# A hybrid attention layer: the input projection as a phase of its own by seven block products, neighbourhood heads first, half of the output projection among the differential units

## The chip, the core and the metric

The kernel runs on one core of a Trainium2 chip. The time is device microseconds (us) of one execution. The engines are named as in the profile: PE (TensorE matmul), PEld (its weight load), DVE (VectorE), ACT (ScalarE), POOL (GpSimd) and SP (SyncE, which here issues every DMA).

## What is computed

One layer on 1024 tokens of width 1024, in float32: a SwiGLU block, a mixer of two kinds of attention heads, a second SwiGLU block, each with a residual and a layer norm. The change is in the mixer.

```python
def hybrid_mixer(h, w_in, w_out, ...):            # h: (1, 1024, 1024), w_in: (1024, 3072)
    p = h @ w_in
    na_q, na_k, na_v, df_q, df_k, df_v = jnp.split(p, splits, axis=-1)      # 512 columns each
    na_out = neighbourhood_attention(na_q, na_k, na_v, na_rpb)   # 8 heads of 64, 16 x 64 token grid,
                                                                 # 8 x 16 window, bias table per head
    df_out = differential_attention(df_q, df_k, df_v, lam, ...)  # 4 heads, softmax1 - lam * softmax2 over
                                                                 # all 1024 keys, ALiBi, RMS norm
    return jnp.concatenate([na_out, df_out], axis=-1) @ w_out    # w_out: (1024, 1024)
# layer: x = LN1(a*x + 0.5*SwiGLU_1(x)); x = LN2(a*x + hybrid_mixer(x)); x = LN3(a*x + 0.5*SwiGLU_2(x))
```

## The kernel before

Every large product is made of three matmuls on a value split into a high and a low part (hi x hi, hi x lo, lo x hi; `mm3`, and L568 to L570 in the projection). `split` makes the two parts: a cast on ACT (L66) and a subtraction on DVE or POOL (L67). The layer-normed x lies transposed in `xq` as four blocks (A11, A12, A21, A22: two halves of tokens by two halves of the width).

The kernel runs through these stages. `gate_up` (first SwiGLU) takes 22 column tiles: for most of them it uses seven block products of 4 k-steps (Strassen-Winograd: 7 x 12 = 84 matmuls of 512 columns) in place of eight (96). `down_phase` follows and ends in row blocks (`Rows.down`, 24 matmuls, layer norm and 8 transposes into `xq` for each of 8 row blocks).

Then the mixer. Its heads form eight groups of 128 columns: four differential ("df") heads, then four pairs of neighbourhood ("na") heads. `project(g)` makes K, V and Q of one group by plain products: 3 matrices x 2 token halves x 24 = 144 matmuls, 1152 in all. It is a generator that stops after each 3 matmuls. The first group's projection runs alone; the other seven are fed by `Filler` into the units of the group before, so that 3 matmuls of the next group stand at each `fill()` in the program. A df unit is one block of 128 queries of one head (32 units): `df_scores` (8 matmuls, two additions with a row minimum on DVE at L682, two exponentials on ACT, a reciprocal and two combinations on DVE), `df_transpose` (8 transposes, casts and subtractions) and, for each two units, `df_out` (24 matmuls of 256 columns, a norm). An na unit is 128 queries of a pair of heads (32 units): `na_scores` (4 matmuls, L822 on DVE, exponentials on ACT, a scaling on POOL at L828), two units later `na_transpose` (6 transposes), three units later `na_out` (12 small matmuls). The bias tables are loaded by `na_raw` (16 DMAs per group) and built by `na_tables` (12 POOL instructions per group, L793). V is transposed on PE (`df_v` L663, `na_v` L803). In the last na group there is nothing left to project, and the units run without filler; the loads of the output weights and of the attention outputs (`load_o`) are issued in it.

The output projection follows: attention outputs come back from DRAM (`oTd`), 8 k-steps, 384 matmuls, in two passes over the row blocks, the second with LN2. Then the second SwiGLU.

The program is ordered per engine ahead of time: buffers come from pools that are opened and closed with the stages, an instruction waits when its buffer is still read by an earlier stage that used the same memory, and each engine and the SP queue takes its list in order.

## Time and profile before

| | |
|---|---|
| Runs (median, lowest, highest of 3) | 1962.92, 1962.77, 1968.08 us |
| Profiled execution: time, span | 1969.43 us, 1967.7 us |
| PE, DVE, ACT, POOL busy in the span | 1926.4 (98%), 1217.6 (62%), 762.3 (39%), 208.8 (11%) us |
| Matmul instructions in the span | 9152 |
| DMA, busy share of 16 engines | 39.3% on the queue that SP issues to |

Busy time is the union of an engine's instructions. Matmuls overlap, so that the time of one (some 390 ns for 512 columns) is longer than the step from one to the next; the step is read from the starts in the timeline. The stages of the mixer begin at about 679 us (first projection alone), 712.6 (df units), 1003.4 (na units) and 1205.3 us (output projection).

### The profile page before, as it was taken

To read this page: it belongs to the slowest core of one execution; us is meant where nothing else is said; L and a number is where in the kernel's file an instruction comes from. 1 tells how busy PE (TensorE), PEld (TensorE's weight loads), DVE (VectorE), ACT (ScalarE), POOL (GpSimd) and SP (SyncE) were. 2 spreads that over 40 slices of the span, in tenths; PEclk is the share of its full clock that TensorE was granted. 3 is DMA by queue.
4 is the path that set the end of the run, shared out by engine and by line. 5 is a ranking of instruction groups with operands and counts; after the bars stand their busy time and mean duration, and the time that the engine had idled before them with its cause. 6 is when DMAs were issued, how large, how long until landed. Compare 5 with 4: busy or idle time off the path is not lost.

```text
span 1967.7 us, 24088 instructions
## 1 busy us (share of the span) xinstructions
PE 1926.4 (98%) x9152; PEld 1562.2 (79%) x9152; DVE 1217.6 (62%) x1823; ACT 762.3 (39%) x1228; POOL 208.8 (11%) x188
## 2 busy tenths in 40 slices
PE   9999999999999999999999999999999999999998
PEld 7777887877887878888777777887787888878887
DVE  8575655545555956778663346787666646455557
ACT  5333333334333245556544455133333333344331
POOL 0000000000001312011044443100000000000005
PEclk9999999999999999999999999999999999999999
DMA  4556323248762331112122226224555222387632
GB/s 168 208 203 222 120 102 118 102 166 300 235 196 88 106 91 41 49 41 62 30 56 67 64 65 226 83 89 160 192 205 191 93 102 99 125 294 254 195 119 86
DMA packets 90771, 266.26 MB, mean 135 GB/s; under 512 B 11680, under 2 KB 15648, under 8 KB 82976
## 3 DMA queue, kind: packets, MB, share of 16 engines
q1 hardware_dynamic: 90656, 264.73, 39.3%
q8 instruction: 72, 1.18, 0.2%
q14 instruction: 43, 0.35, 0.1%
HBM read 183.42 MB, written 72.88 MB: 130 GB/s over the span
## 4 chain that ended last, share of the span: by engine, by line
PE 42%; DMA 3%; DVE 3%; ACT 1%; issue 1%; POOL 0%; SPq 0%; POOLq 0%; DVEq 0%; ACTq 0%
PE psA L80 5%; PE psA L82 5%; PE psA L81 5%; PE psA L435 5%; PE psB L435 4%; PE psB L80 3%; PE psB L81 3%; PE psB L82 3%; PE psB L568 2%; PE psB L570 2%; PE psB L569 2%; PE psB L851 2%; PE psA L818 1%; DMA wr<-in_wgu 1%; PE psB L843 1%
## 5 line engine op out<-in xcount | busy, mean ns | idle before, releaser
L80 PE MATMUL psA<-x,wsp 128*128 128x512 f32 x448 | 181.5, 405 | 8.8 <-ACT t L377 5.3
L80 PE MATMUL psA<-s,wsp 128*128 128x512 f32 x480 | 189.6, 395 | 0.0
L82 PE MATMUL psA<-s,wsp 128*128 128x512 f32 x480 | 187.4, 390 | 0.0
L81 PE MATMUL psA<-s,wsp 128*128 128x512 f32 x480 | 186.7, 389 | 0.0
L66 ACT CAST wsp<-wr 128x1024 fp32r<-128x1024 f32 x124 | 128.9, 1049 | 128.9 <-DVE wr L205 121.3
L81 PE MATMUL psA<-x,wsp 128*128 128x512 f32 x448 | 175.8, 392 | 0.5 <-DVE x L67 0.5
L82 PE MATMUL psA<-x,wsp 128*128 128x512 f32 x448 | 175.1, 391 | 0.0
L568 PE MATMUL psB<-x,wsp 128*128 128x512 f32 x384 | 160.5, 418 | 0.0
L67 DVE TENSOR_TENSOR wsp<-wr,wsp 128x1024 fp32r<-128x1024 f32 x124 | 149.5, 1223 | 12.9 <-ACT wsp L66 12.9
L570 PE MATMUL psB<-x,wsp 128*128 128x512 f32 x384 | 152.2, 396 | 0.0
L569 PE MATMUL psB<-x,wsp 128*128 128x512 f32 x384 | 150.9, 393 | 0.0
L67 POOL TENSOR_TENSOR wsp<-wst,wsp 128x1024 fp32r<-128x1024 f32 x28 | 67.6, 2415 | 759.3 <-ACT wsp L66 759.3
L67 DVE TENSOR_TENSOR hd<-wst,hd 128x1024 fp32r<-128x1024 f32 x84 | 102.0, 1223 | 73.0 <-ACT hd L66 68.2
L204 DVE TENSOR_TENSOR wr<-wr 128x1024 f32<-128x1024 f32 x40 | 49.0, 1225 | 148.6 <-DMA wr<-in_wgu 148.6
L66 ACT CAST hd<-wst 128x1024 fp32r<-128x1024 f32 x84 | 87.7, 1054 | 124.7 <-PE psA L435 36.3
L66 ACT CAST wsp<-wst 128x1024 fp32r<-128x1024 f32 (+1 forms) x90 | 93.0, 1034 | 105.5 <-DMA wst<-in_wd 27.9
L67 DVE TENSOR_TENSOR wsp<-wst,wsp 128x1024 fp32r<-128x1024 f32 (+1 forms) x62 | 73.8, 1190 | 84.1 <-ACT wsp L66 76.0
L80 PEld LDWEIGHTS psA<-x,wsp 128*128 128x128 f32 x448 | 84.1, 188 | 45.4 <-ACT t L377 16.1
L435 PE MATMUL psA<-hd 128*128 128x512 f32 x504 | 116.2, 389 | 0.0
L144 POOL TENSOR_TENSOR mv<-mv,cols 128x1 f32<-128x1 f32 x24 | 35.5, 1478 | 721.1 <-DVE mv L143 721.1
L435 PEld LDWEIGHTS psA<-hd 128*128 128x128 f32 x504 | 94.6, 188 | 19.7
L80 PEld LDWEIGHTS psA<-s,wsp 128*128 128x128 f32 x480 | 90.0, 188 | 25.4 <-ACT sg L394 8.2
(183 smaller groups left out, 4096.4 us busy)
## 6 DMA issues: line engine op xcount, KB each, us to landing
wr<-in_wgu SPq DMA_DIRECT2D x42, 1024.0 KB, 4.8
hSd<-hs SPq DMA_DIRECT2D x18, 1792.0 KB, 5.7
wst<-hSd SPq DMA_DIRECT2D x126, 256.0 KB, 3.6
wst<-wTd SPq DMA_DIRECT2D x72, 256.0 KB, 3.7
wst<-in_wd SPq DMA_DIRECT2D x54, 256.0 KB, 4.8
wst<-in_w_in SPq DMA_DIRECT2D x24, 512.0 KB, 3.4
wt<-in_wd SPq DMA_DIRECT2D x18, 512.0 KB, 3.7
wt<-in_wd SPq DMA_DIRECT2D x36, 256.0 KB, 5.4
```

The source lines that it names most:

```text
L66: A.copy(hi, x)
L67: eng.tensor_tensor(lo, x, hi.bitcast(FT), OP.subtract)
L80: T.matmul(ps, ah, bh, start=start and j == 0, stop=False, skip_group_check=skip)
L81: T.matmul(ps, ah, bl, start=False, stop=False, skip_group_check=skip)
L82: T.matmul(ps, al, bh, start=False, stop=j == n - 1, skip_group_check=skip)
L144: G.tensor_tensor(mv[:, 3:4], mv[:, 2:3], mhalf[:, 0:1], OP.pow)
L204: V.tensor_tensor(l[:, 0:4:3], l[:, 2:4], l[:, 3:5], OP.subtract)
L435: T.matmul(banks[T_], o[:, x, a], o[:, w, 512:1024], start=start and p == 0 and j == 0, stop=p == NP - 1 and j == 2, skip_group_check=not ...
L568: T.matmul(ps, hi, xh, start=k == 0, stop=False)
L569: T.matmul(ps, hi, xl, start=False, stop=False)
L570: T.matmul(ps, lo, xh, start=False, stop=k == KT - 1)
L851: T.matmul(po[64 * j:64 * j + 64, c % 2], Vc[0:w, r + k, 64 * j:64 * j + 64], PTs[j][0:w, k], start=k == 0, stop=k == 2)
```

## The change

All of K, V and Q is projected first, into DRAM. The gate-up code becomes a class `Seven` that takes what to do with its results; `KQ` runs it over 8 column tiles (K as the "gate" and Q as the "up" of each group: 2 plain tiles of 96 and 6 of 84 matmuls) and writes hi and lo parts to `kqd`. V follows in seven products of 48 matmuls with x as the stationary operand, so that it comes out with tokens on the partitions; its weight sums are made among the KQ tiles (`wVd`), the results go to `vdd` (hi and lo, df heads) and `vnd` (na heads). `project`, both transposes of V and `oTd` go.

The four na groups run before the four df heads. They have no filler. K, Q and V are loaded from DRAM (`load_k` 4 DMAs per group, `load_q` 8, `na_v` 16, `load_v` 2). Attention outputs are split at once into the blocks of `xq`, which the projection no longer needs. The na half of the output projection (`out_na`, 64 pieces of 3 matmuls, with the residual) is the filler of the df units; its sums go to DRAM as `x1e`. The output stage then has the 4 k-steps of the df heads, 192 matmuls.

```diff
-    oTd = dr.tile([8, P, S], FT, name="oTd")
+
+    x1e = dr.tile([8, P, DM], FT, name="x1e")
+    kqd = [dr.tile([P, 2, 2, 2, 512], FT, name=f"kqd{h}") for h in range(8)]
+    wVd = dr.tile([P, 4, 4, 512], FT, name="wVd")
+    vdd = dr.tile([P, 2, 8, 512], FT, name="vdd")
+    vnd = dr.tile([S, 512], FT, name="vnd")
...
+        def put(s, f, j, t, x):
+            o = s.c.dv.tile([P, 2, 512], FR, name="dv")
+            hi, lo = o[:, 0], o[:, 1]
+            if j == 0:
+                A.activation(hi, x, AF.Copy, scale=k_scale(f))
+                V.scalar_tensor_tensor(lo, x, k_scale(f), hi.bitcast(FT), OP.mult, OP.subtract)
+            else:
+                if f < 4:
+                    x, hi, lo = by_columns(x), in_order(hi), in_order(lo)
+                split_back(hi, lo, x)
+            dma(kqd[f][:, j, :, t], o.bitcast(FT))
...
+        def plain(s, f, t, ps):
+            for j in range(2):
+                s.put(f, j, t, ps[:, j])
+
+        def add(s, f, j, t, x, ps):
+            to = s.c.u[:, t] if j else s.c.sg[:, t]
+            V.tensor_tensor(to, x, ps, OP.add)
+            s.put(f, j, t, to)
+
...
+            if f == 7:
+                s.ops.append(fetch_v(len(s.ops)))
+            elif i == 4 and 1 <= f < 5:
+                l = s.wt.tile([P, 7, 512], FT, name="wt")
+                dma(l[:, 1:5], I["wv"].rearrange("p (b k c) -> p b k c", b=4, k=4)[:, :, f - 1])
+                sum4(l)
+                for b, x in enumerate((l[:, 0:1], l[:, 3:4], l[:, 5:7])):
+                    dma(wVd[:, b:b + x.shape[1], f - 1], x)
...
+    W0, load0 = first_weights(I["wkq"])
+    for j in range(2):
+        for k in (0, 4):
+            load0(j, k, 4)
+    with ExitStack() as es:
+        c = Seven(es, 2)
+        kq = KQ(c)
+        c.run(I["wkq"], 8, kq, W0, None, kq.begin, kq.hook)
+        ops = kq.ops
...
+        def put_df(t, T_, x):
+            o = c.dv.tile([P, 2, 512], FR, name="dv")
+            split_back(o[:, 0], o[:, 1], x)
+            dma(vdd[:, :, 4 * t + T_], o.bitcast(FT))
+
+        def put_na(t, x, banks):
+            for T_ in range(4):
+                o = wst.tile([P, 1024], FT, name="wst")[:, 0:512]
+                V.tensor_tensor(o, x[T_], banks[T_], OP.add)
+                dma(vnd[(4 * t + T_) * P:(4 * t + T_ + 1) * P], o)
+
+        A_ = [psA.tile([P, 2, 512], FT, name="psA") for _ in range(2)]
+        A_ = [x[:, i] for x in A_ for i in range(2)]
+        product(0, A11, A_, True)
+        p1 = copies(A_, [c.t() for _ in range(4)])
+        B_ = four()
+        product(1, A12, B_, True)
+        for T_ in range(4):
+            V.tensor_tensor(p1[T_], p1[T_], B_[T_], OP.add)
+            put_df(0, T_, p1[T_])
+        product(2, c.S2, A_, False)
+        u2 = copies(A_, [x[:, i] for x in (c.u, c.sg) for i in range(2)])
+        C_ = four()
+        product(3, A21, C_, True)
+        p5 = copies(C_, [c.t() for _ in range(4)])
+        product(4, c.S3, A_, False)
+        put_na(1, p5, A_)
+        product(5, c.S4, C_, False)
+        put_na(0, u2, C_)
+        product(6, A22, A_, False)
+        for T_ in range(4):
+            put_df(1, T_, A_[T_])
...
-            wk, wv, wq = (split_w(I["w_in"][c]) for c in (ck, cv, cq))
...
-        PIECES = 48
-        groups = [dict(kind="df", h=h) for h in range(4)] + [dict(kind="na", h=h) for h in range(4)]
-
-        def filler(i, places):
-            return Filler(project(groups[i]) if i < 8 else nothing(), PIECES, places)
...
+        def load_k(g):
             K = g["K"] = kp.tile([P, 2, S], FR, name="K")
...
+            for j in range(2):
+                a, b = slice(64 * j, 64 * j + 64), slice(64 - 64 * j, 128 - 64 * j)
+                for to, i in ((a, 0), (b, 1)):
+                    dma(K[to, j].bitcast(FT).rearrange("p (t c) -> p t c", t=2), kqd[g["f"]][a, 0, i])
+
+        def load_q(g, t):
+            Q = qp.tile([P, 2, 2, 512], FR, name="Q")
+            g["Q"].append(Q)
+            for j in range(2):
+                a, b = slice(64 * j, 64 * j + 64), slice(64 - 64 * j, 128 - 64 * j)
+                for to in (a, b):
+                    dma(Q[to, j].bitcast(FT), kqd[g["f"]][a, 1, :, t])
...
+            def na_v(g, c):
+                c0, nc_, _ = NA_C[c]
+                Vc = vp.tile([P, 4, P], FT, name="Vc")
+                rows = vnd.rearrange("(r c) d -> r c d", c=GW)
+                for k in range(4):
+                    dma(Vc[0:4 * nc_, k], rows[4 * k:4 * k + 4, c0:c0 + nc_, g["h"] * P:(g["h"] + 1) * P])
+                return Vc
...
+                        if r == 1 and c == 3:
+                            for t in range(2):
+                                split(*xk(t, g["h"]), g["oT"][:, t * 512:(t + 1) * 512], V)
...
+            g = groups[0]
+            na_raw(g)
+            na_tables(g, 0, V)
+            load_q(g, 1)
+            for i in range(4):
+                g, nxt = groups[i], groups[i + 1]
+                g["oT"] = op_.tile([P, S], FT, name="oT2")
+                g["V"] = g["V"] if i else [na_v(g, c) for c in range(4)]
+                wo.append(split_w(I["w_out"][i]))
+                for r in range(2):
+                    tabs = g["tab"]
+                    for c in range(4):
+                        es_ = na_scores(g, r, c, tabs)
+                        if c == 1:
+                            if r == 0:
+                                na_tables(g, 1)
+                                if i < 3:
+                                    na_raw(nxt)
+                                load_k(nxt)
+                                load_q(nxt, 0)
+                            elif i < 3:
+                                na_tables(nxt, 0)
+                        if r == 1:
+                            if i < 3:
+                                nxt.setdefault("V", []).append(na_v(nxt, c))
+                            if c == 2:
+                                load_q(nxt, 1)
+                        queue.append(dict(g=g, r=r, c=c, e=es_, V=g["V"][c], age=-1))
+                        advance()
+            while queue:
+                advance()
...
+            def load_v(g):
...
+                for i in range(2):
+                    dma(Vt[:, i].bitcast(FT), vdd[:, i, :, g["h"] * P:(g["h"] + 1) * P])
...
-                    dma(oTd[4 + g["h"], :, qq * 256:(qq + 1) * 256], oT)
+                    o = slice(qq % 2 * 256, qq % 2 * 256 + 256)
+                    hi, lo = (x[:, o] for x in xk(qq // 2, 4 + g["h"]))
+                    split(hi, lo, oT, V)
...
+            def out_na():
+
+                for tb in range(8):
+                    y = yt.tile([P, DM], FT, name="yt")
+                    dma(y, x1d[tb])
+                    for dh in range(2):
+                        ds_ = slice(dh * 512, (dh + 1) * 512)
+                        ps = psB.tile([P, 512], FT, name="psB")
+                        for k in range(4):
+                            (ah, al), w = o_part(k)(tb), wo[k]
+                            for j, (x, i) in enumerate(((ah, 0), (ah, 1), (al, 0))):
+                                T.matmul(ps, x, w[:, i, ds_], start=k == 0 and j == 0, stop=k == 3 and j == 2)
+                            if k == 3:
+                                V.scalar_tensor_tensor(y[:, ds_], y[:, ds_], ALPHA, ps, OP.mult, OP.add)
+                                if dh:
+                                    dma(x1e[tb], y)
+                            yield
...
+            units = [(g, qb) for g in groups[4:8] for qb in range(8)]
...
+            load_v(groups[4])
+            fill = Filler(out_na(), 64, 92)
...
-            dma(m.y[t], x1d[t])
-            if t < 4:
-                load_o(4 + t)
-                wo.append(split_w(I["w_out"][src[4 + t]], wo_p, "wo", V if t == 1 else G))
+            dma(m.y[t], x1e[t])
+        wo = [split_w(I["w_out"][4 + k], *((wo_p, "wo") if k > 1 else ())) for k in range(4)]
...
-        hs = [o_part(k) for k in range(8)]
-        m.down(hs[0:2], wo[0:2], ALPHA)
-        m.down(hs[2:8], wo[2:8], 1.0, post2)
+        m.down([o_part(4 + k) for k in range(4)], wo, 1.0, post2)
```

## Rows read from the trace of the kernel before

**Rows 1.** Busy time by stage: us, PE, PEld, DVE, ACT, POOL; clock, DMA share, GB/s.
```profile
640.00:679.00 39.00, 39.00 (x217) 33.77 (x217) 37.46 (x64) 8.68 (x14) 9.34 (x7) 0.98 0.23 89
679.00:712.60 33.60, 33.60 (x155) 27.94 (x154) 12.25 (x18) 9.18 (x15) 10.50 (x5) 1.00 0.46 133
712.60:1003.40 290.80, 285.44 (x1566) 236.12 (x1566) 213.53 (x453) 170.97 (x336) 42.18 (x28) 1.00 0.17 49
1003.40:1205.30 201.90, 195.88 (x1196) 152.89 (x1194) 94.71 (x286) 100.72 (x279) 92.75 (x116) 0.98 0.26 74
1205.30:1307.00 101.70, 101.70 (x520) 86.20 (x519) 71.40 (x111) 18.78 (x30) 18.99 (x11) 1.00 0.35 127
```

**Rows 2.** Timeline of PE, row blocks, and first product after the output stage: start, us.
```profile
647.53 0.39 PE L82 MATMUL psB<-hd,wsp 128*128 128x512 f32 x1
...
652.32 0.39 PE L82 MATMUL psB<-wsp,hd 128*128 128x512 f32 x1
652.55 1.03 PE L161 MATMUL psA<-ident,y 128*128 128x128 f32 x8
...
658.89 1.04 PE L161 MATMUL psA<-ident,y 128*128 128x128 f32 x8
...
1300.20 0.47 PE L80 MATMUL psA<-x,wsp 128*128 128x512 f32 x1
```

**Rows 3.** Timeline, second gate-up: PE's wait at its entry; one DVE addition, two tiles apart.
```profile
1364.03 0.50 PE L80 MATMUL psA<-x,wsp 128*128 128x512 f32 x1 [1.24 <-DVE u L386]
...
1551.15 0.68 DVE L373 TENSOR_TENSOR sg<-t,psB 128x512 f32<-128x512 f32 x1
...
1589.94 0.68 DVE L373 TENSOR_TENSOR sg<-t,psB 128x512 f32<-128x512 f32 x1
```

**Rows 4.** Groups on DVE, df stage: shapes, count, busy us, mean ns, idle before.
```profile
L682 DVE CUSTOM_DVE_ANT_0 e<-psA,dist 128x1024 f32<-128x1024 f32 x64 | 76.9, 1220 | 1.0
L689 DVE SCALAR_TENSOR_TENSOR e<-e,st 128x1024 f32<-128x1024 f32 x32 | 45.2, 1414 | 1.0
L700 DVE TENSOR_TENSOR aT<-psB,aT 128x512 fp32r<-128x512 f32 x63 | 41.8, 685 | 1.9 <-ACT aT L699 1.8
L604 DVE TENSOR_TENSOR Q<-psB,Q 64x512 fp32r<-64x512 f32 x18 | 12.3, 686 | 12.0 <-ACT Q L603 11.9
L582 DVE SCALAR_TENSOR_TENSOR K<-psB,K 64x512 fp32r<-64x512 f32 x16 | 11.0, 688 | 5.4 <-ACT K L581 5.0
...
L666 DVE TENSOR_TENSOR Vt<-psB,Vt 128x512 fp32r<-128x512 f32 x8 | 5.2, 685 | 0.0
```

**Rows 5.** Timeline of DVE: the reciprocal of the first and the third df unit.
```profile
719.98 0.17 DVE L687 RECIPROCAL st<-st 128x2 f32<-128x2 f32 x1 [1.19 <-ACT e L685]
...
733.22 0.17 DVE L687 RECIPROCAL st<-st 128x2 f32<-128x2 f32 x1
```

**Rows 6.** Groups on POOL and the weight cast on ACT, na stage.
```profile
L828 POOL TENSOR_SCALAR pe<-pe,st,cols 128x264 f32<-128x264 f32 (+3 forms) x64 | 38.6, 613 | 76.0 <-DVE st L826 69.9 <-PE psA L818 4.2 <-PE psB L843 1.9
L793 POOL TENSOR_TENSOR tab<-mask,raw 128x288 f32<-128x288 bf16 (+3 forms) x42 | 32.3, 802 | 13.0 <-DVE st L822 11.5 <-DVE oT L729 1.4
L67 POOL TENSOR_TENSOR wsp<-wst,wsp 128x1024 fp32r<-128x1024 f32 x9 | 21.4, 2381 | 11.2 <-ACT wsp L66 11.2
...
L66 ACT CAST wsp<-wst 128x1024 fp32r<-128x1024 f32 x9 | 9.4, 1045 | 1.0 <-DMA wst<-in_w_out 1.0
```

**Rows 7.** Timeline of DVE: reciprocals of the last group's first and eighth na unit.
```profile
1179.06 0.17 DVE L826 RECIPROCAL st<-st 128x2 f32<-128x2 f32 x1 [0.23 <-ACT pe L824]
...
1200.70 0.17 DVE L826 RECIPROCAL st<-st 128x2 f32<-128x2 f32 x1 [0.62 <-ACT pe L824]
```

**Rows 8.** Timeline of PE at the na stage's start, and the clock there (busy columns as in Rows 1).
```profile
1017.39 0.81 PE L818 MATMUL psA<-K,Q 128*128 128x264 f32 x2 [2.89 <-DVE st L822]
...
1014.00:1020.00 6.00, 3.11 (x12) 2.38 (x11) 5.50 (x13) 1.79 (x6) 3.66 (x5) 0.75 0.23 49
```

**Rows 9.** Timeline of SP: eleven DMA issues in a row.
```profile
687.00 5.64 SPq L645 DMA_DIRECT2D raw<-in_rpb  x11
```

More of the change, by code (lines that the diff above doesn't have):

```diff
@@ new lines, in tile_hybrid_layer, with product, four, copies @@
+    W0, load0 = first_weights(I["wkq"])
+    for j in range(2):
+        for k in (0, 4):
+            load0(j, k, 4)
+    with ExitStack() as es:
+        c = Seven(es, 2)
+        kq = KQ(c)
+        c.run(I["wkq"], 8, kq, W0, None, kq.begin, kq.hook)
+        ops = kq.ops
+        def product(i, x, banks, start):
+            for p in range(4):
+                while len(ops) < min(14, 2 * i + p // 2 + 5):
+                    ops.append(fetch_v(len(ops)))
+                o, cs = ops[2 * i + p // 2], slice(p % 2 * 512, p % 2 * 512 + 512)
+                for T_ in range(4):
+                    a = slice(T_ * P, (T_ + 1) * P)
+                    for j, (y, w) in enumerate(((0, 0), (0, 1), (1, 0))):
+                        T.matmul(banks[T_], x[:, y, p, a], o[:, w, cs], start=start and p == 0 and j == 0,
+                                 stop=p == 3 and j == 2, skip_group_check=not start)
+        def four():
+            return [psB.tile([P, 512], FT, name="psB") for _ in range(4)]
+        def copies(banks, to):
+            for x, ps in zip(to, banks):
+                A.copy(x, ps)
+            return to
+        def put_df(t, T_, x):
[26 more added lines that the diff above has]
+        product(6, A22, A_, False)
+        for T_ in range(4):
+            put_df(1, T_, A_[T_])
```

571 lines of the change are left out of this document (254 added, 317 removed).

## The prediction

> **What bounds the kernel now.** I read the busy time by stage first [rows 1]. PE is busy for all of 33.6 us in the first projection, 285.4 of 290.8 us among the df units, 195.9 of 201.9 among the na units and all of 101.7 in the output stage. DVE is busy for 213.5 us of the df stage (73%) and less elsewhere. So PE sets the pace in the whole mixer, and it does so in the two attention stages because projection products fill what the attention leaves free. The steps come from the timeline [rows 2]: 21 products of 512 columns lie between 647.53 and 652.32, so one takes 0.228 us, though its own row says 0.39. A row block of 24 products and 8 transposes takes 658.89 - 652.55 = 6.34 us.
>
> The stretch that the change rewrites runs from the first projection product at 679.0 to the first product of the second SwiGLU at 1300.2 [rows 1, 2]: 621.2 us. What lies outside is the same work. I build the new stretch piece by piece against this. The sum is a difference, so it is made against the profiled execution (1969.43 us, span 1967.7, so 1.7 us lie around the span) and carried over to the median of the runs, 1962.9, which lies 6.5 us lower.
>
> **What leaves and what comes on PE.** The projection had 1152 products; now K and Q take 2 x 96 + 6 x 84 = 696 and V takes 7 x 48 = 336, in all 1032. That is 120 fewer: 27 us. 96 transposes of V leave as well. A transpose costs (6.34 - 24 x 0.228) / 8 = 0.11 us [rows 2], so this is some 10 us. Were PE still the bound everywhere, the change would give 37 us. But the products that leave the attention stages were their cover: by the code 576 (four groups) in the df stage and 432 (three) in the na stage. Only 192 (the na half of the output projection) come back, all to the df units.
>
> A rule of the Trainium skill speaks against the change here: Perfetto Trace Analysis, Optimization Strategy, says of kernels whose most-contended engine changes over time that "performance may be improved by interleaving those regimes". The old stages are such an interleaving, and the trace agrees (PE 98% busy beside DVE at 73% in the df stage).
>
> **Projection phase.** 1032 x 0.228 = 235.3 us. The same loop runs 38.79 us for two tiles in the second SwiGLU [rows 3], 19.40 each where 84 products need 19.15, so 6 tiles add 1.5. At its entry PE waits 1.24 us at once and a few such times more [rows 3]; I take 4. The first block of x is covered by 48 products (10.9 us) and no longer by 72, with the weight splits moved from POOL to a DVE that is busy 37.5 of 39 us there [rows 1]: 2. The changes of banks in the V products: 2. Sum 245 us; bounds 240 (half of these waits) and 254 (twice them). The stores (2 MB per tile) and the V weight sums I cost at nothing: the DMA share was 0.46 at most [rows 1], and a tile's 19 us of products cover them; if a store held the queue, the next tile's weights behind it would be late, which is inside the upper bound.
>
> **Neighbourhood phase.** The old last group had no filler: its reciprocals go from 1179.06 to 1200.70 for seven steps [rows 7], 3.09 us per unit. POOL alone needs per group 16 scalings, 12 table pieces and one weight split [rows 6]: 16 x 0.61 + 12 x 0.80 + 2.4 = 21.8 us, 2.7 per unit. That is close below 3.09, so V's work leaving PE and DVE helps little. At each head change there is a chain: the tables must be built before the next raw tables may load into the same buffers, `na_raw` then issues 16 DMAs, and behind it on SP stand the next group's K and Q loads and V's 16. SP needs 0.51 us per issue [rows 9], 45 issues per group, 23 us; a group lasts 8 x 3.09 = 24.7. I add 2 us per group for this, and 5 us for the first unit to pass scores, exponential, POOL and transposes with an empty PE. 4 x 26.7 + 5 = 112 us. Bounds: POOL's floor, 4 x 21.8 + 3 = 90, and 4.1 us per unit with the same fill, 136, which is a group that SP and the tables hold up by 8 us.
>
> **Differential phase.** DVE is busy 213.5 us there, of which the projection's K, Q and V splits took 11.0 + 12.3 + 5.2 [rows 4]. That leaves 185. New on DVE are 16 additions of 512 columns (0.69 each, as L700) and 16 low parts of 256 columns (not in the trace: between half of 0.69 and all of it; I take 0.4): 17.4. So 202 us, 6.3 per unit. PE: 285.4 - 576 x 0.228 - 32 x 0.11 + 192 x 0.228 = 194 us, 6.1 with its old stalls. The bound passes to DVE, with PE right behind it. The first units show the pace: reciprocals one and three are 13.24 us apart [rows 5], 6.6 per unit, with DVE almost without gaps. I take 6.6; bounds 6.3 (DVE's floor) and 7.4 (DVE 85% busy: it waits for the exponential where nothing else is ready). The first reciprocal comes some 5 us after the first scores; after the last one follow the combination (1.4), 8 transposes, casts and 24 products of 256 columns, some 7.3. 5 + 31 x 6.6 + 7.3 = 217 us; bounds 208 and 242.
>
> **Output stage.** Half of it is gone: 8 x 6.34 = 50.7 us, as in the first SwiGLU's row blocks, where DVE is just as full as PE [rows 1]. Before it, the last output weight lies where the last df V still is: its cast and subtraction, 1.05 + 2.4 us [rows 6], start after the last df product. 3.6, less 2.0 of products that can run meanwhile. 52.3 us; bounds 50 and 58. DVE ends later behind PE, so the second SwiGLU's first sums may wait: 2 us (0 to 5).
>
> **The clock.** At the na stage's start PE waited 2.89 us, and the granted clock over 1014 to 1020 was 0.75 [rows 8], so about half of these 6 us ran at the lower level, 1.2 GHz. With gaps at the head changes and seams I allow five such falls at 1.5 us: 7; bounds 0 and 40.
>
> The sum: 245 + 112 + 217 + 52.3 + 2 + 7 = 635.3 us against 621.2, **+14 us**: 1983 for the profiled execution, **1977 us** for the median. The 37 us saved on PE are more than spent where PE now idles: its na work is 195.9 - 432 x 0.228 - 64 x 0.11 = 90 us of 112, its df work 194 of 217, and the rest goes at the seams.
>
> **Rivals.** (1) The order that is written ahead overlaps the phases and heads, as old df and na units overlapped without a gap. Then the seams go: 5 (first na unit), 8 (head changes), 5 (first df unit), 4 (entry), 2 and 2, 7 (clock), 33 us, and the time is 1944. For it: buffers of consecutive phases lie mostly in other memory, so loads may start early. Against it: old na units show waits of 2.9 us at the seam even with filler [rows 8]. It decides for "faster" once more than 20 of the 33 us go.
>
> (2) The clock stays low in the na phase, not in five falls only. The phase has 90 us of PE work, 2.8 per unit; at half rate a unit needs 5.6 in place of 3.09. If half of the units run so, 16 x 2.5 = 40 us in place of 7: 2010. For it: [rows 8]. Against it: in the last group PE went on with short gaps at this pace. The Trainium skill states the same danger (TensorE: Matmul & The Clock Gate, HAM oscillation: idle time of PE between bursts brings the half rate back); the trace agrees in that one place.
>
> (3) SP bounds the na phase: with one wait for buffers per group of the size of the tables' 9.6 us [rows 6], a group takes 23 + 9.6 = 32.6 us, and the phase 24 us more: 2001.
>
> (4) That the change does not do what it says, fewer products, is excluded by the code.
>
> **How the numbers follow.** Forecast 0.50, its own range 1963 to 1996; rival 1 0.28; rival 2 0.12; rival 3 0.10. 0.3%, 6 us, is what a measurement of this kernel can tell from no change: the sides part at 1957 and 1969. Faster: 0.26 of rival 1 and 0.02 of the forecast, 0.28. Same: 0.10 of the forecast, 0.02 of rival 1, 0.02 of the others, 0.14. Slower: 0.58. The range reaches from 1940 (rival 1 a little beyond) to 2010 (rivals 2 and 3); the lowest and highest bounds of all pieces at once lie outside.
>
> **What would show it.** PE near 98% in the projection phase of 245 us, then about 80% among both kinds of units, DVE over 90% among the df units; reciprocals 3.1 to 3.4 us apart in the na phase and 6.6 in the df phase; the output stage some 52 us long. The prediction is wrong if na units follow each other in 2.7 us, if df units take over 7.4 us, or if the na phase begins with a gap of more than 10 us for its tables and V.

## The result, and the profile after

The change makes the kernel slower: 2034.5 us (median of 4 runs, 2032.4 to 2036.2) against 1965.4 (1962.8 to 1968.1) in the same measurement. The ratio is 1.035, 95% interval 1.033 to 1.037. The forecast was slower, but 1977 with a range to 2010. The profiled execution takes 2034.17 us, its span is 2032.4.

Busy time by stage, kernel after, the columns of [rows 1]: the end of the first SwiGLU, K and Q, V, the wait for the first scores, the neighbourhood ("na") units, the differential ("df") units, the output stage.

```profile
640.00:668.20 28.20, 28.20 (x168) 24.80 (x167) 27.92 (x47) 4.70 (x8) 5.82 (x4) 1.00 0.21 82
668.20:825.70 157.50, 151.00 (x659) 121.48 (x658) 113.48 (x126) 59.08 (x80) 1.46 (x1) 1.00 0.63 212
825.70:913.10 87.40, 87.40 (x384) 71.59 (x384) 35.02 (x42) 25.57 (x35) 5.60 (x6) 1.00 0.51 162
913.10:929.40 16.30, 0.41 (x2) 0.00 (x0) 3.37 (x8) 4.29 (x6) 2.34 (x1) 0.58 0.74 226
929.40:1072.70 143.30, 116.97 (x716) 83.86 (x717) 57.23 (x232) 72.61 (x219) 73.25 (x103) 0.80 0.68 146
1072.70:1304.20 231.50, 199.09 (x1140) 162.73 (x1138) 194.23 (x443) 136.63 (x284) 15.13 (x17) 0.96 0.43 121
1304.20:1365.10 60.90, 53.80 (x276) 44.56 (x275) 48.36 (x84) 13.13 (x24) 15.67 (x10) 0.95 0.22 79
```

Against the terms of the forecast:

| stage | forecast, us | measured, us | more |
|---|---|---|---|
| up to the first projection product | 679.0, as before | 668.2 | -10.8 |
| projection | 245 | 244.9 | -0.1 |
| na units, first wait and clock | 112 + 7 | 16.3 + 143.3 | +40.6 |
| df units | 217 | 231.5 | +14.5 |
| output stage to the second SwiGLU | 52.3 + 2 | 60.9 | +6.6 |
| second SwiGLU to the end | 667.5, as before | 667.3 | -0.2 |

The sum is +50.6; 1983 and 50.6 are the 2034 of the profiled execution. Four fifths of the excess lie in the na stage and the wait before it. No engine is busy there for more than 82% of the time, and the DMA share is 0.68 where the old na units had 0.26 [rows 1].

What happens where the first na head ends and the second begins: SP's, POOL's and PE's timeline of the kernel after (start, us from start to end of the group, engine, line, operation, count, idle time before and its releaser).

```profile
951.28 3.38 SPq L730 DMA_DIRECT2D K<-kqd  x4
954.71 2.56 SPq L738 DMA_DIRECT2D Q<-kqd  x4
957.32 11.41 SPq L807 DMA_DIRECT2D Vc<-vnd  x12
968.83 2.88 SPq L738 DMA_DIRECT2D Q<-kqd  x4
971.75 4.22 SPq L807 DMA_DIRECT2D Vc<-vnd  x4
976.47 0.36 SPq L71 DMA_DIRECT2D wst<-in_w_out  x1
977.64 10.42 SPq L783 DMA_DIRECT2D raw<-in_rpb  x16
988.16 2.43 SPq L730 DMA_DIRECT2D K<-kqd  x4
```

```profile
953.21 9.34 POOL L798 TENSOR_TENSOR tab<-mask,raw 128x264 f32<-128x264 bf16 x12
967.35 1.11 POOL L831 TENSOR_SCALAR pe<-pe,st,cols 128x264 f32<-128x264 f32 x2 [4.80 <-DVE st L829]
```

```profile
955.88 1.80 PE L854 MATMUL psB<-PT,Vc 128*64 128x128 f32 x24
962.32 1.36 PE L821 MATMUL psA<-K,Q 128*128 128x264 f32 x4 [4.64 <-DMA Q<-kqd]
```

SP is at its list all the time, with no pause of over 1.3 us: from K of the second head (951.28) to K of the third (988.16) one round of its list takes 36.9 us, where [rows 9] gave 0.51 us per issue and 23 us per head. V's 16 issues take 15.6 us of it, the tables' 16 take 10.4, the gaps between them counted in. The issues themselves are 26.4 us of the round; the other 10.5 are gaps, 7.7 of them waits for transfers. The trace's records show SP's issues on eight semaphores in turn, and an issue that waits does so until the transfer eight places ahead of it has landed. SP's longest waits over the stage (us in all, times, longest; L807 issues V, L783 the raw tables):

```profile
SPq L807 <- DMA Vc<-vnd: 5.5, 6, 1.3
SPq L783 <- DMA Q<-kqd: 4.9, 6, 1.1
SPq L807 <- DMA Q<-kqd: 4.4, 7, 0.7
SPq L783 <- DMA Vc<-vnd: 4.1, 12, 0.8
```

The heads follow each other in 32.9, 35.6, 37.1 and 37.7 us, first score to first score. PE has emptied the first head's units at 957.7 and waits for Q; POOL makes all 12 table pieces in one block that ends at 962.55, within 0.3 us of Q. So two arms reach this head change together. PE's waits over the stage; the longest of the first line is the wait before the stage:

```profile
PE psA L821 <- DMA Q<-kqd: 33.4, 13, 15.9
PE psB L846 <- POOL pe L831: 1.7, 4, 1.1
```

Within the stage PE idles for 26.3 us, and 17.5 of them (33.4 less 15.9) are waits for Q's loads: 5.9 at this head change, 0.3 and 3.4 at the two others, the rest inside the heads.

### The profile page after: what moved, and what is told of

Same layout as the page of the kernel before. It is cut to its first block, busy times and chain, and to the rows that moved or that the text cites. A ratio compares the mean times of both kernels' runs of the same rounds, so it can differ in the third digit from the quotient of the medians.

```text
span 2032.4 us, 23987 instructions
## 1 busy us (share of the span) xinstructions
PE 1920.7 (95%) x8924; PEld 1546.0 (76%) x8924; DVE 1285.2 (63%) x1898; ACT 772.0 (38%) x1218; POOL 153.9 (8%) x165
## 5 line engine op out<-in xcount | busy, mean ns | idle before, releaser
L80 PE MATMUL psA<-x,wsp 128*128 128x512 f32 x560 | 226.5, 404 | 13.0 <-ACT t L344 9.0
L81 PE MATMUL psA<-x,wsp 128*128 128x512 f32 x560 | 220.3, 393 | 0.9 <-DVE x L67 0.9
L82 PE MATMUL psA<-x,wsp 128*128 128x512 f32 x560 | 219.1, 391 | 0.0
L80 PE MATMUL psA<-s,wsp 128*128 128x512 f32 x552 | 218.4, 396 | 0.4 <-DVE dv L573 0.4
L82 PE MATMUL psA<-s,wsp 128*128 128x512 f32 x552 | 215.2, 390 | 0.0
L81 PE MATMUL psA<-s,wsp 128*128 128x512 f32 x552 | 214.8, 389 | 0.0
L66 ACT CAST wsp<-wr 128x1024 fp32r<-128x1024 f32 x144 | 149.7, 1049 | 139.1 <-DVE wr L210 128.5
L67 DVE TENSOR_TENSOR wsp<-wr,wsp 128x1024 fp32r<-128x1024 f32 x144 | 173.5, 1222 | 14.0 <-ACT wsp L66 13.8
L67 DVE TENSOR_TENSOR wsp<-wst,wsp 128x1024 fp32r<-128x1024 f32 (+1 forms) x80 | 93.3, 1171 | 105.9 <-ACT wsp L66 102.1
L209 DVE TENSOR_TENSOR wr<-wr 128x1024 f32<-128x1024 f32 x46 | 56.3, 1224 | 161.2 <-DMA wr<-in_wgu 149.3
L80 PEld LDWEIGHTS psA<-x,wsp 128*128 128x128 f32 x560 | 105.6, 188 | 56.8 <-ACT t L344 21.6
L385 DVE TENSOR_TENSOR u<-t,psA 128x512 f32<-128x512 f32 x80 | 54.8, 685 | 137.9 <-ACT t L351 84.6
L66 ACT CAST wsp<-wst 128x1024 fp32r<-128x1024 f32 (+1 forms) x86 | 86.9, 1012 | 135.4 <-DMA wst<-in_wd 29.3
L80 PEld LDWEIGHTS psA<-s,wsp 128*128 128x128 f32 x552 | 103.6, 188 | 30.4 <-ACT sg L390 8.2
L82 PEld LDWEIGHTS psA<-x,wsp 128*128 128x128 f32 x560 | 105.6, 189 | 22.8
L81 PEld LDWEIGHTS psA<-x,wsp 128*128 128x128 f32 x560 | 105.8, 189 | 22.1 <-DVE x L67 2.8
L82 PEld LDWEIGHTS psA<-s,wsp 128*128 128x128 f32 x552 | 103.6, 188 | 22.6
L81 PEld LDWEIGHTS psA<-s,wsp 128*128 128x128 f32 x552 | 103.7, 188 | 20.2
```

The source lines that it names most:

```text
L66: A.copy(hi, x)
L67: eng.tensor_tensor(lo, x, hi.bitcast(FT), OP.subtract)
L80: T.matmul(ps, ah, bh, start=start and j == 0, stop=False, skip_group_check=skip)
L81: T.matmul(ps, ah, bl, start=False, stop=False, skip_group_check=skip)
L82: T.matmul(ps, al, bh, start=False, stop=j == n - 1, skip_group_check=skip)
L209: V.tensor_tensor(l[:, 0:4:3], l[:, 2:4], l[:, 3:5], OP.subtract)
```

## The experiments

Three theories went in. A is the third rival: SP's ordered list of issues bounds the na stage. B is the second: the lower clock does. C: the transfers themselves do. Unless an interval is given, a time is that of a single execution; the kernel before took 1966.0 to 1972.4 us on the same chips. Totals of single executions differ by several us in parts that an edit doesn't touch (`e12_half`, 2022.2 us, is 12 below the change, of which its stage holds 1.3), so stages are compared. "Na" is the time from the first na to the first df score. Its own scatter shows in `e13_nofill`, whose edit is in the df units and whose na stage takes 140.5 us in place of 143.3: a difference of up to 3 us says nothing. The df units of the runs that don't touch them take 230.2 to 232.6 us, `e15_kqmerge` apart. The diffs are shortened.

**Fewer issues (A).** `e1_raw` loads each raw bias table in one DMA; `e1_raw_v` also stores V so that a block is one load (16 issues per head become 4).

```diff
-  for r8 in range(8):
-      dma(raw[r8 * 16:(r8 + 1) * 16], src)            # 16 x 466
+  dma(raw, src)                                       # ap [[NCOL, 8], [1, 16], [1, RAW]]
-  for k in range(4):
-      dma(Vc[0:4 * nc_, k], rows[4 * k:4 * k + 4, c0:c0 + nc_, ...])
+  dma(Vc[0:4 * nc_], vnd[g["h"], :, c0:c0 + nc_])     # e1_raw_v: vnd is [4, 4, GW, 4, P]
```

> The raw bias tables of a head are loaded by one DMA in place of eight (16 issues per group become 2; bytes and rows are the same). A, the list of DMA issues on SP bounds the na phase: 14 x 0.45 us less per group, the phase some 25 us shorter, near 2009 us. B, PE's low clock bounds it: no change, 2034. C, the transfers themselves (many 512 B rows of V) bound it: no change, 2034.

> As e1_raw, and V of the na heads lies in DRAM so that one DMA loads a column block (4 issues per group in place of 16, runs of 2 KB in place of 512 B; 8 more stores in the V products). A: 26 issues less per group, 14 us, more than the phase can use: groups of about 25 us in place of 33 to 37, near 2000 us. B: no change. C: less as well, but then e1_raw alone gives nothing.

2022.5 and 2022.6 us; na 135.2 and 134.2. Of 44 load issues per head 14 and 26 are gone, and the stage gains 8 and 9 us. So the number of issues has a share, a small one: once SP's list is shorter, something else of nearly the same length is behind it. PE's waits in `e1_raw` show what:

```profile
PE psA L820 <- DMA Q<-kqd: 17.9, 2, 17.2
PE psB L845 <- POOL pe L830: 12.2, 10, 4.7
```

Behind the first score PE waits 0.7 us for Q's loads, where it was 17.5, and 12.2 us for POOL's scalings, where it was 1.7.

**The clock (B).** `e2_warm` puts four products of 512 columns that nobody reads behind each na unit. Later, `e14_warm2` put 16 of them ahead of the first scores of each half head, and `e12_half` left out one of two score products.

```diff
+  pw = psB.tile([P, 512], FT, name="psB")
+  for i in range(4):                                  # e14_warm2: range(16), where c == 0
+      T.matmul(pw, wo[0][:, 0, 0:P], wo[0][:, 0, 0:512], start=i == 0, stop=i == 3)
```
```diff
-  for i in range(2):                                  # e12_half
-      T.matmul(ps[:, j, 0:nk], g["Q"][r][:, j, i, ...], Kg[...], start=i == 0, stop=i == 1)
+  T.matmul(ps[:, j, 0:nk], g["Q"][r][:, j, 0, ...], Kg[...], start=True, stop=True)
```

> Four products of 512 columns that nobody reads are added to each na unit (0.9 us of PE at the full clock), so that PE is busier; nothing else changes. B: the granted clock of the na phase rises from 0.80 towards 1 and the time falls by 15 to 30 us. A and C: the clock rises and the time stays within 6 us, or grows a little by the added work.

> Eight times, ahead of the first scores of each half head, PE makes 16 products of 512 columns that nobody reads (3.7 us at the full rate, 29 us in all), where it waits for loads anyway. If the lower clock that follows these waits costs time, the units behind them run at the full rate and the phase falls by 8 us or more from 143; if it costs nothing, the phase stays or grows by the part of the 29 us that no wait covers.

> The second of the two score products of each half unit is left out (the low parts of Q, so the scores are rounded): 64 products of 264 to 384 columns, some 9 us of PE work at the full rate and 11 at the mean clock of this phase. If PE's rate at the lower clock is on the path, the phase falls by 9 to 14 us from 143; if the phase waits for loads and PE merely runs slowly while it waits, by 3 us or less, and PE's idle time grows by what it saves.

The na stage by window (columns as above), `e2_warm`, `e14_warm2`, `e12_half`:

```profile
929.00:1071.50 142.50, 133.05 (x839) 99.88 (x839) 58.69 (x232) 72.00 (x219) 73.26 (x103) 0.92 0.67 148
```
```profile
930.80:1072.50 141.70, 125.95 (x830) 95.19 (x829) 61.78 (x232) 71.49 (x219) 71.91 (x103) 0.94 0.65 144
```
```profile
926.60:1068.60 142.00, 106.41 (x653) 75.51 (x654) 56.44 (x232) 71.97 (x219) 73.19 (x103) 0.76 0.67 146
```

The clock rises from 0.80 to 0.92 and 0.94, and the stage stays at 142 (2030.6, 2032.5 and 2022.2 us in all). `e2_warm` alone proves little, since its own products take 29 us; `e12_half` does the rest: PE has 10.6 us less to do, and idles 9.3 us more. PE's rate is not on the path here. B falls: beside loads that come late, the low clock is a mark of the waits and costs no more than the scatter of 3 us.

**Loads left out (C).** Heads 1 to 3 use head 0's V (`e3_vonce`), its K and Q (`e6_kqonce`), or V, K, Q and raw tables (`e7_allonce`).

```diff
-  nxt.setdefault("V", []).append(na_v(nxt, c))
+  nxt.setdefault("V", []).append(groups[0]["V"][c])   # e3, e7
-  load_k(nxt)
-  load_q(nxt, 0)
+  nxt["K"], nxt["Q"] = groups[0]["K"], groups[0]["Q"] # e6, e7 (loads kept for the first df head)
-  na_raw(nxt)
+  nxt["raw"] = groups[0]["raw"]                       # e7
```

> V of the na heads is loaded for the first group only and used for all four (output differs): 48 issues and 7,168 rows of 512 B less. A: 48 x 0.7 us off SP's list, the phase some 25 to 33 us shorter, near 2005. C: the same or more. B: no change.

> Heads 1 to 3 of the neighbourhood phase use head 0's K and Q tiles, so 24 loads (3 MB per head) and their issues are gone; V, tables and weights are loaded as before (the output is that of other K and Q). If the volume of transfers bounds the phase, 9 MB less is worth more than the 2.7 MB of V that gave 27 us: the phase falls from 143 to 112 us or less. If it is V's own 16 transfers of 512-byte rows that come late, whatever else is on the way, the phase gains under 10 us: 135 or more. If SP's issues bound it, 8 of some 45 issues per head are gone, 4 to 5 us per head: about 128.

> Heads 1 to 3 use head 0's V, K, Q and raw tables (the output is not that of the reference); only the output weights and the loads for the first differential head are left. This is the floor that the engines alone set. If transfers and issues are the whole of the excess, the phase is 100 to 105 us (8 units of 3.09 us per head, and a first unit). If a chain of waits among DVE, ACT, POOL and PE has a share, it stays at 112 or more.

2005.3, 2004.0 and 1996.8 us. The na stage, `e3_vonce`, `e6_kqonce`, `e7_allonce`:

```profile
930.00:1045.90 115.90, 101.54 (x716) 75.17 (x717) 56.04 (x232) 71.92 (x219) 73.54 (x103) 0.90 0.72 158
```
```profile
931.30:1045.80 114.50, 102.18 (x716) 75.39 (x717) 57.11 (x232) 71.91 (x219) 73.02 (x103) 0.91 0.42 101
```
```profile
932.90:1038.70 105.80, 96.87 (x705) 70.77 (x705) 54.91 (x231) 68.44 (x215) 69.03 (x101) 0.95 0.32 72
```

Either load left out gives 27 to 29 us, all of them 37.5: not a sum, but a floor. 105.8 us is what the engines need in the lists of `e7_allonce`, with the first unit's fill, and this is the forecast's 112 less 6. It is not the bytes as such either: V is 0.9 MB per head, K and Q 3 MB, and both give the same.

**Sooner, or from another queue.** `e10_early0` asks for K and Q of the next head at the first unit of a head, ahead of its tables, and for V at units 3 to 6; `e9_early` does the same with the loads of `e1_raw_v`. `e8_vact` issues V's loads from ACT.

```diff
+  if r == 0 and c == 0:
+      load_k(nxt); load_q(nxt, 0)
+  if i < 3 and 2 <= 4 * r + c < 6:
+      nxt.setdefault("V", []).append(na_v(nxt, 4 * r + c - 2))
...                                                   # the old places of these calls go
```
```diff
-  dma(Vc[0:4 * nc_, k], rows[...])
+  A.dma_start(Vc[0:4 * nc_, k], rows[...])            # e8_vact
```

> All transfers are kept, but in the text of the kernel the next head's K and Q are asked for at the first unit of a head (before its raw tables), its V at units 3 to 6, and tables and V go in 2 and 4 issues per head. So far V left out gives 27 us, K and Q left out 29, all left out 37.5, fewer issues 9. If lateness of the loads in SP's list is the cause, the same bytes asked for sooner give most of it: the phase takes 108 to 118 us. If the bytes themselves are the cause, or engine lists that empty a head's units before the next head's scores whatever the loads do, it stays at 130 or more.

> As the run before, with the 16 issues for raw tables and 16 for V per head as they were: only the places are changed. If the place in SP's list decides, the phase falls to 125 or less; if the number of issues does (over 45 per head of 0.4 to 1 us each, 33 to 37 us per head), it stays at 135 to 145, and the raw tables are what is late now.

> All 64 loads of V of the neighbourhood heads are issued from ScalarE's queue, so they stand in no list behind waits for K, Q and tables. If SP's ordered list delays V, the phase gains most of what leaving V out gave: 116 to 125 us. If the transfers themselves, or V's stream of short rows, are the cause, it stays at 138 to 145; ScalarE's issues may cost a little.

Na 139.1, 149.4 and 161.2; 2034.6, 2037.4 and 2050.9 us. None gives the gain that was asked of it, and `e10_early0` and `e8_vact` end above both of their ranges. Asking for the same loads sooner moves the wait and doesn't remove it: the heads of `e10_early0` follow in 28.4, 44.4, 35.8 and 40.9 us. On ACT it is worse, likely because ACT's list holds the exponentials too (argued, not shown).

**POOL's tables.** `e11_tabonce` builds the four tables once; the raw tables are still loaded.

```diff
-  na_tables(g, 1)
+  if i == 0: na_tables(g, 1); tab1 = g["tab"]
+  g["tab"] = tab1
-  na_tables(nxt, 0)
+  nxt["tab"] = tab0
```

> Heads 1 to 3 use head 0's four tables (the output is that of another bias); the raw tables are loaded as before but not read, so 36 of 48 table pieces, 29 us, leave POOL, and no load waits for a table. If POOL's block of 12 pieces between two heads (9.6 us) holds the units up, the phase falls by 20 us or more; if K, Q and V come late in SP's list, by 10 or less.

2029.3 us, na 142.3, with POOL busy 45.6 us in place of 73.3. With the loads as they are, POOL's arm alone is not the cause.

**The pattern of a load.** `e15_kqmerge` merges K's and Q's pairs of 64-partition loads, on top of `e1_raw_v`, with Q stored in the order that this needs; `e16_rows` is `e1_raw_v` with V in 16 loads of whole rows.

```diff
-  for to, i in ((a, 0), (b, 1)):
-      dma(K[to, j]..., kqd[g["f"]][a, 0, i])
+  dma(K[:, j]..., src)                                # e15: ap [[hi to lo, 2], [row, 64], ...]
-  for to in (a, b):
-      dma(Q[to, j]..., kqd[g["f"]][a, 1, :, t])
+  dma(Q[:, j]..., src)                                # e15: ap [[0, 2], [row, 64], [1, 1024]]
```
```diff
-  dma(Vc[0:4 * nc_], vnd[g["h"], :, c0:c0 + nc_])
+  for r in range(4):                                  # e16
+      dma(Vc[r * nc_:(r + 1) * nc_], vnd[g["h"], r, c0:c0 + nc_])
```

> All bytes are kept, but K goes in 2 loads and Q in 2 per half (128 partitions each, in place of 4 of 64), V in 4 and the raw tables in 2: 12 transfers per head in place of 44. With tables and V alone so merged the phase was 134 us. If the number of transfers, or their 64 partitions, is the cause, it falls to 115 or less, and the differential phase gains a little too; if the bytes are, or the lists of the engines, it stays at 130 or more.

> As the run with tables in 2 and V in 4 loads per head (134 us), with V in 16 loads again: each is now 24 or 32 whole rows of 2 KB into as many partitions, and no load has an outer dimension of 4. If the loads of a head pass the queue one behind the other, each at the rate that its pattern gets (K and Q 3 MB at 215 GB/s, 14.6 us; the output weight 2.4; V 4.3 in place of 9.5 to 12.8; tables 2), a head needs 23 to 26 us of transfers, less than the 26.5 us that the engines need, and the phase falls to 108 to 118. If the number of transfers or their bytes decide, it is 134 or more, as 12 issues per head come back.

`e15_kqmerge` is the largest miss of the study: 2289.3 us, na 285.5, from 12 transfers of the same bytes. Windows while one form of load has the queue: kernel after, Q alone (first row) and V alone (second); `e15_kqmerge`, merged Q; `e16_rows`, V by rows behind the last loads of Q. The last two columns are the DMA share and GB/s.

```profile
929.00:933.00 4.00, 2.15 (x6) 1.44 (x6) 0.78 (x3) 0.61 (x2) 0.20 (x1) 0.50 1.07 215
937.00:944.00 7.00, 6.42 (x41) 4.25 (x41) 4.60 (x23) 5.08 (x18) 4.03 (x7) 1.00 0.30 79
```
```profile
963.00:993.00 30.00, 5.49 (x19) 4.19 (x20) 2.76 (x12) 2.71 (x10) 1.11 (x2) 0.50 0.13 52
```
```profile
936.00:942.00 6.00, 5.42 (x26) 4.10 (x25) 3.64 (x20) 4.39 (x16) 3.81 (x7) 0.73 0.50 118
```

Q by 64 partitions keeps all DMA engines busy (a share of 1.07: the records overlap a little) at 215 GB/s. V's pattern begins with a dimension of 4, has a share of 0.30 and 79 GB/s, so that a load of 64 KB takes 0.8 us, near the 0.95 us from one V issue to the next. The issue itself lasts 0.76 us in this window; in `e6_kqonce`, with less ahead of them in the queue (956.8 to 959.6 us), five of the same issues last 0.51 to 0.52 each. So SP waits behind its own transfers. The merged loads begin with a dimension of 2 and have 0.13, two of sixteen, at 52 GB/s. The Trainium skill states such a rule (DMA: Bandwidth & Descriptors, Why a DMA increments its semaphore by 16 and not by 1): a transfer uses the largest number of engines, up to 16, that divides the slowest dimension of both patterns. The trace agrees with 2 and 16; for 4 it would be 0.25, and the records show 0.30.

By rates, one head passes the queue in 3.1 MB / 215 GB/s + 0.9 MB / 79 GB/s + 0.5 MB / 215 GB/s = 14.4 + 11.4 + 2.3 = 28.1 us (K and Q, V, the output weight). The 10.4 us of the tables' issues lie in part beside it: from 977.64 to 984.05 the DMA share is 0.57, as the last loads of Q and V and the weight still move, and only in the 4.1 us behind it does it fall to 0.26. That is 32 to 38.5 us, about what a head takes. By this estimate A and C are one line of work.

`e16_rows` takes 2022.5 us, na 131.2, where 108 to 118 was expected: 3 us less than `e1_raw_v`, within the scatter. Its window has 118 GB/s and a DMA share of 0.50, so this is no rate of the pattern: V's issues wait for K's and Q's loads, the ones eight places ahead, for 27.5 us in the stage (18.3 for Q, 9.2 for K), and where they don't wait they follow each 0.4 us. Still SP's rounds, from K to K, now take 25.1, 28.1 and 22.9 us, while the heads follow in 27.8, 35.9, 36.0 and 31.5. PE's waits:

```profile
PE psA L821 <- DMA Q<-kqd: 21.3, 2, 20.2
PE psB L846 <- POOL pe L831: 11.6, 9, 4.6
```

Behind the first score 1.1 us are waits for loads, 11.6 for POOL's scalings and 11.3 for DVE. What holds the stage now is in POOL's and PE's timeline at the end of its second head:

```profile
984.13 2.36 POOL L67 TENSOR_TENSOR wsp<-wst,wsp 128x1024 fp32r<-128x1024 f32 x1
986.44 3.91 POOL L799 TENSOR_TENSOR tab<-mask,raw 128x352 f32<-128x352 bf16 x5
990.34 1.14 POOL L831 TENSOR_SCALAR pe<-pe,st,cols 128x288 f32<-128x288 f32 x2
991.45 4.39 POOL L799 TENSOR_TENSOR tab<-mask,raw 128x288 f32<-128x288 bf16 x6
1000.33 1.10 POOL L831 TENSOR_SCALAR pe<-pe,st,cols 128x264 f32<-128x264 f32 x2 [4.49 <-DVE st L829]
```
```profile
990.97 1.52 PE L846 MATMUL psB<-ident,pe 128*96 128x128 f32 x6 [4.61 <-POOL pe L831]
992.41 3.31 PE L854 MATMUL psB<-PT,Vc 128*64 128x128 f32 x24
995.65 1.40 PE L821 MATMUL psA<-K,Q 128*128 128x264 f32 x4
```

No load is waited for here. POOL's list has a weight split and five table pieces ahead of the scaling that PE's transposes wait for, then six more ahead of the next head, and PE's list empties the old head before it scores the new one. In `e7_allonce` the list is another: table pieces stand two to four at a time between scalings.

```profile
981.08 1.55 POOL L798 TENSOR_TENSOR tab<-mask,raw 128x288 f32<-128x288 bf16 x2 [1.27 <-DVE st L825]
982.62 1.30 POOL L831 TENSOR_SCALAR pe<-pe,st,cols 128x384 f32<-128x384 f32 x2
983.89 3.33 POOL L798 TENSOR_TENSOR tab<-mask,raw 128x288 f32<-128x288 bf16 x4
987.22 2.23 POOL L831 TENSOR_SCALAR pe<-pe,st,cols 128x288 f32<-128x288 f32 x4
```

The lists are written ahead of time, and leaving loads out rewrites them too. So `e7_allonce` changes two things, and how much of its gain is transfers and how much is the order of the lists stays open. For `e3_vonce` the trace says more. POOL still makes nine table pieces in a block, but the old head's last scaling stands ahead of it, as it does in the kernel after (952.10, ahead of the block at 953.21):

```profile
985.57 1.58 POOL L831 TENSOR_SCALAR pe<-pe,st,cols 128x288 f32<-128x288 f32 x2
987.12 6.90 POOL L798 TENSOR_TENSOR tab<-mask,raw 128x264 f32<-128x264 bf16 x9
```

So the 27 us of `e3_vonce` are not the breaking up of the block; they speak for the loads. In `e16_rows` this scaling stands behind the weight split and five pieces. That the stage would fall to some 116 us with `e16_rows`' loads and this order of POOL's list is not shown: no run changes the order alone.

**The first wait, and DVE among the df units.** `e45` allocates the projection's staging tiles behind the sums of x, so that K and Q of head 0 may load while V is projected, and moves one subtraction per pair of df units to POOL. `e13_nofill` leaves the na half of the output projection out of the df units.

```diff
-  s.dv = pool("dv", 2) if n == 2 else None
   s.xs = pool("xs", 1)
   s.S2, s.S3, s.S4 = [...]
+  s.dv = pool("dv", 2) if n == 2 else None
...
-  split(hi, lo, oT, V)
+  split(hi, lo, oT, G)
```
```diff
-  (ah, al), w = o_part(k)(tb), wo[k]                  # e13_nofill
-  for j, (x, i) in enumerate(((ah, 0), (ah, 1), (al, 0))):
-      T.matmul(ps, x, w[:, i, ds_], start=k == 0 and j == 0, stop=k == 3 and j == 2)
   if k == 3:
-      V.scalar_tensor_tensor(y[:, ds_], y[:, ds_], ALPHA, ps, OP.mult, OP.add)
```

> Two edits in two stages. (a) The staging tiles of the projection's results are allocated behind the sums of x, so the first loads of K and Q need not wait for the last stores of V: if the 16 us between the last projection product and the first score are that wait for memory, they fall to 6 or less; if they are the time that the data takes to be stored and read back, they stay at 14 to 16. (b) The low part of each pair of differential units is subtracted on POOL in place of DVE: 16 times 0.5 us leave DVE. If DVE paces the differential units, their 231.5 us fall by 6 to 8; if it is the chain of waits around the exponential, by 3 or less.

> The neighbourhood half of the output projection is left out: 192 products (44 us of PE) and 16 additions of 512 columns (11 us of DVE) leave the differential units; the rows of x are still loaded and stored (the output lacks these heads). If DVE paces the units, the phase falls from 231.5 by some 11 us to 220. If PE's products delay the units' own transposes and scores, it falls by 20 us or more. If the chain of one unit through the exponential sets it, by 5 or less.

`e45`: 2022.6 us. The wait falls from 16.3 to 1.8 us, and the na stage grows from 143.3 to 157.4: the second head's scores begin at 960.6 in place of 962.3, although the first head's began 16 us sooner. Ahead of these scores PE waits 4.8 us for V's loads and 0.8 for Q's. That is the clearest sign for the loads: each head starts when its loads are there. The df units, `e45` and `e13_nofill`:

```profile
1070.70:1297.70 227.00, 198.49 (x1140) 163.50 (x1139) 191.16 (x428) 137.13 (x284) 28.54 (x32) 0.97 0.43 124
```
```profile
1067.30:1294.20 226.90, 176.96 (x960) 138.98 (x959) 189.46 (x428) 134.96 (x286) 16.97 (x17) 0.90 0.36 94
```

With `e45` DVE is busy for 3.1 us less, and the stage is 4.5 shorter. With `e13_nofill` the 16 additions (10.9 us) and 192 products (44 us at 0.228) are gone, DVE is busy for 4.8 us less, and the stage is 4.6 shorter. So the filler's products on PE cost these units little: 20 us or more was expected if they did. That DVE paces the units isn't shown: by the ranges set before, 4.6 us speak for the chain of waits (5 or less, against 11), and the 4.5 of `e45` lie between the two (3 or less, 6 to 8). DVE is busy for only 194 of 231.5 us in the kernel after, 84%. This is the head of its list of waits among the df units (us in all, times, longest):

```profile
DVE e L942 <- PE psA L939: 10.9, 15, 1.6
DVE rr L983 <- POOL rr L981: 8.9, 12, 0.9
DVE aT L960 <- ACT aT L959: 4.4, 8, 1.9
```

**The first SwiGLU.** `b1_split` is the kernel before, with the weight splits of its first projection on DVE.

```diff
-  wk, wv, wq = (split_w(I["w_in"][c]) for c in (ck, cv, cq))
+  wk, wv, wq = (split_w(I["w_in"][c], eng=V if g is groups[0] else G) for c in (ck, cv, cq))
```

> The kernel before, with the three weight splits of its first projection on DVE in place of POOL, as the change does for its own first weights. The part up to the first projection product ended 10.8 us sooner after the change, and two waits at 457.8 and 638.2 us were gone. If the splits on POOL made the second wait (POOL's power in the norm stands behind one), about 5 us of it go here, and the first product comes at 674; if the order of allocation in the new block-product class did it, it stays at 679.

1966.3 us beside 1970.5. The first projection product comes at 674.7 us, and the wait of 3.07 us at 638.24 is gone. The other, at 457.8, is still there. 4.2 us is less than two single executions can tell apart, but the trace shows where they come from.

**All mended.** `c2` is `e16_rows` with both edits of `e45`.

> The run before, with the staging tiles behind the sums of x (K and Q of head 0 are loaded while V is projected) and the low part of each pair of differential units on POOL. Seam and neighbourhood phase together took 159.6 us; by the theory of the queue they take 112 to 125, the differential phase 227: 1980 to 1993 us, which is the forecast for the change as such (1977) within its terms. If the theory is wrong they stay at 150 or more, and the time at 2015 or above.

2012.0 us (2010.2 to 2016.1, 4 runs) beside 1969.5; ratio 1.022 (1.020 to 1.024). First wait 5.4 us, na 147.0, df 225.7. The df part is as expected; the first wait and the na stage, 152.4 us, are not: mending the transfers' patterns doesn't give the na stage back. PE's longest waits there are for POOL's scalings (14.8 us) and DVE (11.4), as in `e16_rows`.

## Why the prediction was right in direction and wrong in size

**Right.** The projection phase: 245 forecast, 244.9 measured, PE 97% busy. The engines' work of the na units: 3.09 us per unit and 112 in all, where without loads the stage takes 105.8. The sign, and its reason: work that was saved on PE is lost where PE idles. The rule of the Trainium skill that stood against the change (Perfetto Trace Analysis, Optimization Strategy) agrees with the sign: the kernel with the interleaved stages is faster by 69 us, the cost of the new loads included.

**The step that failed** is "2 us per group" for the change of heads, in the sum for the neighbourhood phase. It took SP's 0.51 us per issue [rows 9], put 23 us of issues beside 24.7 us of units, and let them run side by side. A round of SP's list takes 36.9 us, because an issue waits for the transfers ahead of it: from one to the next V's take some 0.98 and the tables' 0.65 us. PE waits 17.5 us for loads within the stage; with V's loads left out the stage is 27 us shorter, with all of them 37.5. The third rival named the place and had the right size for a head, 32.6 us against 33 to 38, with a chance of 0.10. Its mechanism was another: it had SP wait for table buffers, and no such wait stands in SP's list; what SP waits for is its own queue, V's and Q's loads alike (11.8 us each from 930 to 1060). I had costed V's 16 loads as issues, and never asked at which rate their pattern moves. Right behind SP stand POOL's block of 12 table pieces and a list that empties each head, so that shortening SP's arm alone gives 9 to 12 us and not 37: PE then waits 10 to 12 us for POOL.

**The first rival** is out: the seams did not go away but cost more than forecast, 16.3 us ahead of the first score, and up to 37.5 us of the na stage go with its loads (`e7_allonce`).

**The first wait** of 16.3 us had no term of its own: the 5 us in the sum are the first unit's way through the engines. The forecast named a gap of over 10 us there as a sign that it is wrong. PE waits for Q of head 0, whose loads SP issues from 924.51 us on, behind V's last stores (918.11 to 920.30), a weight and a raw table; `e45` shows that starting the scores sooner doesn't help.

**The clock.** The second rival's place was right: the granted clock is 0.80, and PE's work stretches to 117 us from some 92 at the full rate (an estimate from `e7_allonce`: 96.9 us at 0.95). Its price was not: 25 us of slower PE cost no more than 1 or 2, less than the scatter. The rule of the Trainium skill named with it (TensorE: Matmul & The Clock Gate, HAM oscillation) describes the fall well; here PE isn't what the stage waits for.

**The df units** were mis-sized: 7.0 us per unit where 6.6 was taken, from the first units with the old filler [rows 5]. DVE's work was sized well, 194 us against 202, but the mechanism (DVE paces, over 90% busy) is not borne out: DVE is busy for 84%, and 37 us of short waits between the engines, the longest of them above, make the rest. **The output stage** was mis-sized too, by 6.6 us: PE waits 4.1 us, in two waits, for a norm and 2.1 for POOL's weight splits.

**Before the change's stretch** 10.8 us came back, in a part that I had called the same work: 4.3 of them because the first projection weights are no longer split on POOL, in front of the norm's power. The other 6.5, most of them at the wait at 457.8 us, are not explained.

**Open** is what the na stage is worth with its loads in time and its lists in a good order at once. The best that was seen is 105.8 us, in `e7_allonce`; that run takes some 1997 us, and still does not beat the kernel before.

## What to carry to other kernels

When a stage loses its filler, cost what the filler had covered on the DMA queue as well: list every load of a round, with the rate that its pattern gets in the trace, and add them up as one line, since one queue takes them in turn. Before a chain of loads, tables and units is called hidden, look for the second arm of the same length; leaving out one load at a time finds the floor, but it also rewrites lists that are ordered ahead. A low clock beside waits is a symptom until a run with less PE work gets faster.

## What was not expected of the hardware

A DMA's pattern sets its rate by more than packet size. 2 KB rows to 64 partitions ran at 215 GB/s; 4 KB rows whose pattern began with a dimension of 2 at 52 GB/s, with a share of 0.13 of the DMA engines; 512-byte rows that began with a dimension of 4 at 79 GB/s, with 0.30. Merging two loads into one made them four times slower. And the issue of a load on SP, some 0.6 us for K and Q, stretches when the transfers ahead are slow: for V from 0.51 us with little ahead in the queue to 0.76 in a row of its kind, and for the merged loads to some 10 us, as long as their 512 KB take at 52 GB/s. Everything behind it in SP's list is late by as much.
